# The opening of a decoder layer on one core: c as eight rows, broadcast through PE into PSUM, and a pinned order of sums, copies and splits

## The chip, the cores and the metric

The kernel runs on one core of a Trainium2 chip. The metric is device time in microseconds (us), the median of several runs. Five engines with queues of their own work side by side: PE (matrix products; its weight loads are listed apart as PEld), DVE (vector work), ACT (activations and copies), POOL, and SP, which only issues DMA transfers here. Matrix products are written into PSUM, which is divided into banks of 128 partitions by 512 float32 values. Everything else lives in SBUF.

## The reference, cut to what matters

One decoder layer over 512 tokens of width 1024. A conditioning vector c of 1024 values is multiplied by a large matrix, and the result shifts and scales the tokens. The shifted and scaled tokens u are then multiplied by one wide projection:

```python
mod = c @ w_ada + b_ada
sh1, sc1, gt1, sh2, sc2, gt2 = split(mod, 6)
u = x * (1.0 + sc1) + sh1
proj = u @ w_in          # q, k, v of two attention branches, forget logits, branch gates
...                      # two attentions, output projection, LayerNorm, gated MLP, LayerNorm
```

Only the first two parts of mod (sh1 and sc1), u, and the first columns of proj are touched by the change. All inputs and the output are float32.

## The kernel before, in words

The 1024 channels are cut into eight tiles of 128 (KT = 8). A tile j holds channels in the partitions and the 512 tokens in the free dimension. The opening runs a loop over the tiles. For a tile it needs 128 values of sh1 and 128 of sc1, one for each partition. They are sums over 1024 products of c and a row of the transposed w_ada. So c is needed in every partition, as a tile cbc of 128 x 1024.

**Where cbc comes from.** c is loaded as one row, cbr (L101, on SP's queue). PE multiplies a column of ones with it (L194), once for each half e of 512 columns, into the banks grp[0] and grp[1]. ACT copies each bank into a half of cbc (L195). Then PE runs WARM = 10 products of a tile of zeros (L197) into grp[5], whose results nobody uses.

**The first tile, j = 0.** SP issues the halves of wa[0] (rows for sh1) and wa[1] (rows for sc1) in turn (L217), then 384 columns of w1, the projection weights (L218), the tokens xt (L219), and the other 520 columns of w1 (L220). DVE makes four sums (L201; each leaves its total through a second instruction, the read of the accumulator): for each half e, both q = 0 (sh1) and q = 1 (sc1). Then it adds 1.0 to two rows of the biases bcols (L242), and adds halves and bias into modc (L245). ACT makes uh, the float32r part of u, from xt (L271). DVE makes the full u in place in xt (L282), and then ul, what uh leaves of it. The weights are split in the same way: wh by ACT (L90, the helper hi_of) and wl by DVE (L93, the helper lo_of), for j = 0 in two pieces of 384 and 520 columns. first_pad makes the second piece, and a padded tile for the eight forget columns. For j above 0, each sum is over all 1024 columns at once (mod_col), and the tile's weights are split in one piece.

**The products.** first_mm (L305) multiplies a tile's 128 channels with the columns of w1: groups g of 128 columns, each into its bank grp[g], each as three products (wh with uh, wl with uh, wh with ul), and two for the forget columns: 23 products for a tile, all accumulated over the eight tiles. For a tile, groups 0 to 4 come first, ordered by kind of product, and then groups 5 to 7. Groups 0 to 2 need the first 384 columns of w1 alone.

**What sets the order.** Instructions of one engine run in the order in which its queue holds them. SP's queue is in the order of the code. On the others, tc.issue_after(ins) puts what is traced within it behind ins on ins's engine, without a wait of its own on another engine. paced(a, b) makes a wait until b is done. Waits for data, for buffers that come free, and for a bank that another engine is using are set by the framework.

Of the kernel before, what the change touches and what calls it, by code (L numbers as in the profile page):

```python
# [8 lines left out]
F32 = mybir.dt.float32  # L9
F32R = mybir.dt.float32r  # L10
BF16 = mybir.dt.bfloat16
AF = mybir.ActivationFunctionType
ALU = mybir.AluOpType
# [3 lines left out]
P = 128  # L17
T = 512
D = 1024
KT = D // P  # L20
# [9 lines left out]
W1C = 904  # L30
# [12 lines left out]
GS = 7  # L43
SS = 10
GTILES = (3, 5, 7, 8, 12, 16, 20, 24)
WARM = 10
CUT = 5
FILL = (15, 18, 18), (11, 11, 11)


@with_exitstack
def layer_kernel(ctx: ExitStack, tc: tile.TileContext, out, xT, x, cT, crow, wa0, wa1, bcol, bgt, w1, wct, wv, bf,
                 wp, wo, lncol, lnrow, wup, cwb, wdp):
    nc = tc.nc
    ctx.enter_context(tc.manual_schedule(engines={nc.sync.engine}))
    V, S, G, PE = nc.vector, nc.scalar, nc.gpsimd, nc.tensor
# [11 lines left out]
    early = st0.enter_context(tc.tile_pool(name="early", bufs=1))  # L68
# [20 lines left out]
    def hi_of(o, i, scale=1.0):  # L89
        S.activation(o, i, AF.Copy, scale=scale)  # L90
# [6 lines left out]
        return pre.tile(shape, dt, name=s, tag=s)  # L97

    cbc = preset([P, D], F32, "cbc")
    cbr = early.tile([1, D], F32, name="cbr", tag="cbr")  # L100
    nc.sync.dma_start(cbr, crow)  # L101
    cTs = const([P, KT], F32, "cTs")
    bcols = const([P, 4, KT], F32, "bcols")
    bcd = S.dma_start(bcols, bcol)
# [3 lines left out]
    ident = const([P, P], F32, "ident")  # L108
# [80 lines left out]

    fpad = early.tile([P, KT, P], F32R, name="fpad", tag="fpad")  # L190
    G.memset(fl(fpad), 0.0)
    for e in range(2):
        c = slice(e * 512, (e + 1) * 512)
        PE.matmul(grp[e], ones[0:1, :], cbr[:, c], start=True, stop=True)  # L194
        S.activation(cbc[:, c], grp[e], AF.Copy)  # L195
    for n in range(WARM):
        PE.matmul(grp[5], warm[:, 0:P], warm, start=True, stop=True)  # L197

    def mod_sum(w, col, wt, c, e):
        o = modr[:, w, col, e : e + 1]  # L200
        state["read"] = V.scalar_tensor_tensor(wt[:, c], wt[:, c], 1.0, cbc[:, c], ALU.mult, ALU.mult, accum_out=o)  # L201
        return state["read"]

    def mod_col(w, col, wt):
# [4 lines left out]
    def first_load(j):  # L209
        wa = [early.tile([P, D], F32, name=nm("wa"), tag="wa", bufs=5) for _ in range(2)]  # L210
        r = stg.tile([P, 1024], F32, name=nm("raw"), tag="raw", bufs=LOADS)
        xt = z(F32, "xt")
        if j == 0:
            for e in range(2):
                c = slice(e * 512, (e + 1) * 512)
                for q in range(2):
                    nc.sync.dma_start(wa[q][:, c], wa0[j, q][:, c])  # L217
            nc.sync.dma_start(r[:, 0:384], w1[j][:, 0:384])  # L218
            nc.sync.dma_start(xt, xT[j * P : (j + 1) * P, :])  # L219
            nc.sync.dma_start(r[:, 384:W1C], w1[j][:, 384:W1C])  # L220
        else:
            nc.sync.dma_start(wa[0], wa0[j, 0])
            if j == 1:
                nc.sync.dma_start(wa[1], wa0[j, 1])
            nc.sync.dma_start(r[:, 0:W1C], w1[j])
            if j > 1:
                nc.sync.dma_start(wa[1], wa0[j, 1])
            nc.sync.dma_start(xt, xT[j * P : (j + 1) * P, :])
            if j == 6:
                nc.sync.dma_start(cTs, cT)  # L230
                nc.sync.dma_start(bfs, bf)
        pend[j] = [wa, xt, r]

    def first_acc(j):
        wa = pend[j][0]
        if j == 0:
            for e in range(2):
                for q in range(2):
                    s = mod_sum(q, j, wa[q], slice(e * 512, (e + 1) * 512), e)
            with tc.issue_after(s.ins):  # L240
                for q in (1, 3):
                    V.tensor_scalar_add(bcols[:, q, :], bcols[:, q, :], 1.0)  # L242
            for q in range(2):
                raw = modr[:, q, j, :]
                state["modc"] = V.scalar_tensor_tensor(modc[:, q, j : j + 1], raw[:, 0:1], raw[:, 1:2], bcols[:, q, j : j + 1], ALU.add, ALU.add)  # L245
        else:
            mod_col(0, j, wa[0])
            state["modc"] = mod_col(1, j, wa[1])

    def first_split(j):  # L250
        r = pend[j][2]
        h = stg.tile([P, 1024], F32R, name=nm("wh"), tag="wh", bufs=WBUFS)
        l = stg.tile([P, 1024], F32R, name=nm("wl"), tag="wl", bufs=WBUFS)
        hi_of(h[:, 0:W1C if j else 384], r[:, 0:W1C if j else 384])
        pend[j][2:] = [h, l, r]

    def first_pad(j):
# [9 lines left out]
    def first_mod(j):  # L267
        wa, xt = pend[j][0:2]
        sh, sc = modc[:, 0, j : j + 1], modc[:, 1, j : j + 1]
        a, b = z(F32R, "uh"), z(F32R, "ul")  # L270
        u = state["u"] = S.activation(a, xt, AF.Identity, bias=sh, scale=sc)  # L271
        if j:
            h, l, r = pend[j][2:]
            with tc.issue_after(state["modc"].ins):
                state["after"] = lo_of(l[:, 0:W1C], r[:, 0:W1C], h[:, 0:W1C])
            with tc.issue_after(u.ins):
                u = state["u"] = S.activation(xt, xt, AF.Identity, bias=sh, scale=sc)
            with tc.issue_after(state["after"].ins):
                state["after"] = lo_of(b, xt, a)
        else:  # L280
            h, l, r = pend[j][2:]
            ts = V.tensor_scalar(xt, xt, sc, sh, ALU.mult, ALU.add)  # L282
            with tc.issue_after(ts.ins):
                ts = lo_of(l[:, 0:384], r[:, 0:384], h[:, 0:384])
            with tc.issue_after(ts.ins):
                state["after"] = lo_of(b, xt, a)
        with tc.issue_after(u.ins), tc.issue_after(state["after"].ins):
            first_pad(j)
        uh.append(a)
        ul.append(b)  # L290
# [1003 lines left out]
def _pack(inputs):  # L1294
    import numpy as np

    a = {k: np.ascontiguousarray(v) for k, v in inputs.items()}
    c = np.ascontiguousarray
    w_in, w_ada = a["w_in"], a["w_ada"]
    wk = w_ada.reshape(KT, P, 6, D)  # L1300
    r = {}
    r["xT"] = c(a["x"][0].T)
    r["x"] = a["x"][0]
    r["cT"] = c(a["c"][0].reshape(KT, P).T)
    r["crow"] = a["c"]
    wt = c(w_ada.T).reshape(6, KT, P, D)
    r["wa0"] = c(wt[0:2].transpose(1, 0, 2, 3))
    kf = wk[:, :, [2, 5]].reshape(4, 2, P, 2, 2, 512).transpose(3, 4, 0, 2, 1, 5).reshape(2, 8, P, D)
    r["wa1"] = c(np.concatenate([kf[0], wt[3], wt[4], kf[1]], axis=0))
    bm = a["b_ada"].reshape(6, KT, P)  # L1310
    r["bcol"] = c(bm[[0, 1, 3, 4]].transpose(2, 0, 1))
    r["bgt"] = c(a["b_ada"].reshape(6, D)[[2, 5]])
    def col(kind, n):
        if kind in ("sb", "fox"):
            return (4104 if kind == "sb" else 3080) + n * P
        br, p = PAIRS[n]
        return 1544 * br + 512 * "qkv".index(kind) + p * P

    first = [w_in[:, s : s + P] for s in [col("q", 0), col("k", 0)] + [col("sb", j) for j in range(NG)]]
    cols = np.concatenate(first + [w_in[:, 1536:1544]], axis=1)  # L1320
    r["w1"] = c(cols.reshape(KT, P, W1C))
    wv = np.stack([w_in[:, 1024:1536], w_in[:, 2568:3080]])
    r["wv"] = c(wv.reshape(2, 4, 2, P, 512).transpose(0, 1, 3, 2, 4).reshape(2, 4, P, D))
    starts = [col(*t) for t in TILES]
    r["wct"] = c(np.stack([w_in[:, s : s + P].reshape(KT, P, P).transpose(1, 0, 2).reshape(P, D) for s in starts]))
    r["bf"] = c(a["b_forget"].reshape(NH, 1))
    wpj = np.stack([a["w_fox_proj"], a["w_sb_proj"]]).reshape(2, 4, P, 4, 2, P)
    r["wp"] = c(wpj.transpose(0, 3, 2, 4, 1, 5).reshape(2, 4, P, D))
    r["wo"] = c(a["w_o"].reshape(KT, P, D))
    r["lncol"] = c(np.stack([a["ln1_g"].reshape(KT, P), a["ln1_b"].reshape(KT, P)]).transpose(2, 0, 1))  # L1330
    r["lnrow"] = c(np.stack([a["ln1_g"], a["ln1_b"], a["ln2_g"], a["ln2_b"]]))
    wu = a["w_up"].reshape(KT, P, 2, FT, P)
    r["wup"] = c(wu.transpose(3, 2, 1, 0, 4).reshape(2 * FT, P, D))
    cwb = np.concatenate([a["conv_w"], a["conv_b"][None]], axis=0).reshape(4, 2, FT, P)
    r["cwb"] = c(cwb.transpose(3, 2, 1, 0).reshape(P, 2 * FT, 4))
    wd = a["w_down"].reshape(FP, 2, P, 2, 512)
    b11, b12, b21, b22 = [wd[:, m, :, n] for m in range(2) for n in range(2)]
    r["wdp"] = c(np.concatenate([b11, b12, b22, b21], axis=2))
    return r


_NAMES = ["xT", "x", "cT", "crow", "wa0", "wa1", "bcol", "bgt", "w1", "wct", "wv", "bf", "wp", "wo", "lncol", "lnrow",
          "wup", "cwb", "wdp"]


# [17 lines left out]
```

## Time and profile before

| What | us |
|---|---|
| Median of three runs | 742.30 |
| The three runs | 742.14, 742.30, 743.58 |
| The profiled execution, as timed | 743.61 |
| Its span, from first to last instruction | 741.8 |

Busy shares of the span: PE 98%, DVE 82%, ACT 53%, POOL 11%. A row of the profile names the engine, the line of the kernel, the operation, what it writes and reads (out<-in), the shape and the count. In a timeline the first two columns are the start and the duration in us, and the brackets at the end hold the idle time ahead of the row and who ended it. Rows that follow each other on one engine and line are merged, with their count behind an x. The end of a matmul is modelled, and includes the time until its result is out, so rows of PE overlap.

### The profile page before, as it was taken

Reading aid. Unit: us, or ns where it says so; the run is one execution under the profiler, and the core shown is the slowest. Engines: PE = TensorE matmul, PEld = TensorE weight load, DVE = VectorE, ACT = ScalarE, POOL = GpSimd, SP = SyncE. Lnnn points to the kernel's source line nnn. Section 1 sums busy time; section 2 is a strip of 40 time slices with the busy share of each in tenths; the row PEclk is TensorE's granted clock in tenths of the full one; section 3 lists DMA queues with packets and bytes.
Section 4 is the critical chain, followed back from the end, with each engine's and each line's share of the span. In section 5 each row is a group of like instructions: output and inputs, shape, how many; then the busy total and the mean of one; then the engine's idle time right before and its main releaser. Section 6 shows DMA issues by size and latency. Waiting matters only on the chain.

```text
span 741.8 us, 9838 instructions
## 1 busy us (share of the span) xinstructions
PE 730.3 (98%) x3444; PEld 608.1 (82%) x3444; DVE 608.6 (82%) x1050; ACT 390.5 (53%) x683; POOL 83.1 (11%) x134
## 2 busy tenths in 40 slices
PE   8999999999999999999999999999999999999995
PEld 5888888888888888888889888888888888888885
DVE  6869789988889886884587899988887797679995
ACT  4567457676976664542055455444454544346550
POOL 1027123525000000000000000000001001000010
PEclk9999999999999999999999999999999999999999
DMA  9943545423413241642062788577888867656733
GB/s 326 404 179 95 190 151 189 143 86 115 171 58 114 73 154 42 218 172 86 1 239 64 223 277 253 188 230 232 251 300 221 263 201 206 213 158 226 225 87 87
DMA packets 45220, 131.95 MB, mean 178 GB/s; under 512 B 5905, under 2 KB 6417, under 8 KB 45170
## 3 DMA queue, kind: packets, MB, share of 16 engines
q1 hardware_dynamic: 38610, 113.66, 44.9%
q0 software_dynamic: 3536, 9.24, 6.6%
q10 hardware_dynamic: 3024, 8.41, 3.1%
q8 instruction: 27, 0.44, 0.2%
q14 instruction: 23, 0.19, 0.1%
HBM read 118.38 MB, written 12.85 MB: 177 GB/s over the span
## 4 chain that ended last, share of the span: by engine, by line
PE 92%; DVE 4%; ACT 2%; DMA 1%; issue 1%; DVEq 0%; ACTq 0%
PE ps L134 18%; PE ps L133 18%; PE ps L132 18%; PE ps L305 5%; PE ps L1092 5%; PE ps L1094 5%; PE ps L1093 5%; PE ps L548 3%; PE ps L530 2%; PE ps L890 2%; PE ps L889 2%; PE ps L891 2%; DVE om L509 1%; PE ps L481 1%; PE ps L482 1%
## 5 line engine op out<-in xcount | busy, mean ns | idle before, releaser
L181 ACT ACTIVATE wh<-raw 128x1024 fp32r<-128x1024 f32 (+1 forms) x105 | 109.2, 1042 | 108.8 <-PE ps L133 36.3
L93 DVE TENSOR_TENSOR wl<-raw,wh 128x1024 fp32r<-128x1024 f32 (+2 forms) x114 | 134.8, 1185 | 30.5 <-ACT wh L181 30.3
L132 PE MATMUL ps<-u2h,wh 128*128 128x512 f32 (+1 forms) x376 | 141.5, 376 | 0.0
L133 PE MATMUL ps<-u2l,wh 128*128 128x512 f32 (+1 forms) x376 | 141.2, 376 | 0.0
L134 PE MATMUL ps<-u2h,wl 128*128 128x512 f32 (+1 forms) x376 | 141.2, 376 | 0.0
L132 PEld LDWEIGHTS ps<-u2h,wh 128*128 128x128 f32 x376 | 70.8, 188 | 13.2 <-issue 0.6
L134 PEld LDWEIGHTS ps<-u2h,wl 128*128 128x128 f32 x376 | 70.8, 188 | 12.8
L133 PEld LDWEIGHTS ps<-u2l,wh 128*128 128x128 f32 x376 | 70.8, 188 | 12.7
L132 PE MATMUL ps<-uh,wh 128*128 128x512 f32 x200 | 78.9, 394 | 0.0
L133 PE MATMUL ps<-ul,wh 128*128 128x512 f32 x200 | 78.2, 391 | 0.0
L134 PE MATMUL ps<-uh,wl 128*128 128x512 f32 x200 | 78.1, 391 | 0.0
L1142 ACT ACTIVATE cv<-ps,cw 128x512 f32<-128x512 f32 x44 | 34.0, 772 | 41.0 <-PE ps L134 34.5
L1143 DVE SCALAR_TENSOR_TENSOR cv<-ps,cw,cv 128x511 f32<-128x511 f32 x44 | 32.7, 744 | 17.2 <-ACT cv L1142 17.2
L134 PEld LDWEIGHTS ps<-uh,wl 128*128 128x128 f32 x200 | 37.5, 188 | 8.5 <-DVE wl L93 0.4
L132 PEld LDWEIGHTS ps<-uh,wh 128*128 128x128 f32 x200 | 37.6, 188 | 7.4
L133 PEld LDWEIGHTS ps<-ul,wh 128*128 128x128 f32 x200 | 37.6, 188 | 7.2
L510 POOL TENSOR_TENSOR pt<-pt,om 128x127 f32<-128x127 f32 (+3 forms) x32 | 41.4, 1306 | 9.8 <-DVE om L509 9.8
L160 POOL DMA_DIRECT2D raw<-in_wdp x10 | 8.9, 890 | 248.2 <-DVE ac L577 182.2
L1144 DVE SCALAR_TENSOR_TENSOR cv<-ps,cw,cv 128x510 f32<-128x510 f32 x44 | 32.7, 743 | 0.3
L1150 ACT ACTIVATE cv<-cv 128x512 f32<-128x512 f32 x22 | 13.9, 631 | 34.5 <-DVE cv L1144 34.5
L509 DVE TENSOR_TENSOR_SCAN om<-om,dg 128x127 f32<-128x127 f32 (+3 forms) x32 | 29.4, 978 | 0.7 <-ACT om L504 0.6
L1094 PE MATMUL ps<-wh,hv 128*128 128x512 f32 x72 | 28.0, 389 | 0.0
(234 smaller groups left out, 1581.7 us busy)
## 6 DMA issues: line engine op xcount, KB each, us to landing
raw<-in_wup SPq DMA_DIRECT2D x44, 512.0 KB, 5.6
raw<-in_wa SPq DMA_DIRECT2D x32, 512.0 KB, 4.5
raw<-in_wct SPq DMA_DIRECT2D x25, 512.0 KB, 4.0
raw<-in_wdp SPq DMA_DIRECT2D x20, 512.0 KB, 5.5
wa<-in_wa SPq DMA_DIRECT2D x14, 512.0 KB, 8.2
raw<-in_wdp SPq DMA_DIRECT2D x22, 256.0 KB, 5.1
raw<-t SPq DMA_DIRECT2D x22, 256.0 KB, 3.9
raw<-in_wdp POOLq DMA_DIRECT2D x10, 512.0 KB, 7.8
```

Of the source, the lines that this page charges most:

```text
L93: state["read"] = V.tensor_tensor(o, i, fl(hi), ALU.subtract)
L132: PE.matmul(ps, wh, ah, start=first, stop=False)
L133: PE.matmul(ps, wh, al, start=False, stop=False)
L134: return PE.matmul(ps, wl, ah, start=False, stop=last)
L181: state["hi"] = S.activation(h[:, 0:cols], r[:, 0:cols], AF.Copy)
L305: PE.matmul(grp[g], w, u, start=j == 0 and n == 0, stop=j == KT - 1 and n == (1 if g == 7 else 2))
L509: V.tensor_tensor_scan(d0, d0, dg[:, 513 - (e - s) : 512][:, ::-1], 0.0, ALU.mult, ALU.max)
L510: G.tensor_tensor(pt[b][:, s : e - 1], pt[b][:, s : e - 1], om[:, s + 1 : e], ALU.mult)
L1092: PE.matmul(ps, ah, bh, start=first, stop=False, skip_group_check=onto)
L1093: PE.matmul(ps, ah, bl, start=False, stop=False, skip_group_check=onto)
L1094: return PE.matmul(ps, al, bh, start=False, stop=last, skip_group_check=onto)
L1142: S.activation(t, ps, AF.Identity, bias=cw[:, n, 3:4], scale=cw[:, n, 2:3])
```

## The change

c is loaded as a tile c8s of eight rows of 128 values (c8), on ACT's queue, ahead of bcols. PE multiplies the k-th column of the identity, repeated 128 times, with the eight rows: that is row k of c8 in every partition, 128 columns of a bank. Eight such products fill grp[0] and grp[1]. The zeros' products are now three before them, five behind them, and three that wait for the third sum of tile 0, eleven in all.

For tile 0 the sums read grp[e] instead of cbc. Their order is q = 0 for both halves, then q = 1 for both. ACT copies a bank to cbc behind the sum of q = 1 that reads the same bank. The two bias rows are added ahead of the sums. The split of the first 384 columns of w1 is put behind the second copy. DVE makes uh for tile 0, right behind modc, and ACT makes the full u in xt. SP issues wa[0] whole, wa[1] in halves, then xt, and the two pieces of w1 behind it.

```diff
-WARM = 10
+WARM = 3, 5, 3
...
-    cbr = early.tile([1, D], F32, name="cbr", tag="cbr")
-    nc.sync.dma_start(cbr, crow)
+    c8s = early.tile([KT, P], F32, name="c8s", tag="c8s")
+    S.dma_start(c8s, c8)
...
-    for e in range(2):
-        c = slice(e * 512, (e + 1) * 512)
-        PE.matmul(grp[e], ones[0:1, :], cbr[:, c], start=True, stop=True)
-        S.activation(cbc[:, c], grp[e], AF.Copy)
-    for n in range(WARM):
-        PE.matmul(grp[5], warm[:, 0:P], warm, start=True, stop=True)
-
-    def mod_sum(w, col, wt, c, e):
+    def heat(n):
+        return [PE.matmul(grp[5], warm[:, 0:P], warm, start=True, stop=True) for _ in range(n)]
+
+    heat(WARM[0])
+    for k in range(KT):
+        o = grp[k // 4][:, k % 4 * P : (k % 4 + 1) * P]
+        m = PE.matmul(o, ident[0:KT, k : k + 1].broadcast_to([KT, P]), c8s, start=True, stop=True)
+    with tc.issue_after(m.ins):
+        heat(WARM[1])
+
+    def mod_sum(w, col, wt, c, e, by=None):
         o = modr[:, w, col, e : e + 1]
-        state["read"] = V.scalar_tensor_tensor(wt[:, c], wt[:, c], 1.0, cbc[:, c], ALU.mult, ALU.mult, accum_out=o)
+        state["read"] = V.scalar_tensor_tensor(wt[:, c], wt[:, c], 1.0, cbc[:, c] if by is None else by, ALU.mult, ALU.mult, accum_out=o)
...
         if j == 0:
+            nc.sync.dma_start(wa[0], wa0[j, 0])
             for e in range(2):
                 c = slice(e * 512, (e + 1) * 512)
-                for q in range(2):
-                    nc.sync.dma_start(wa[q][:, c], wa0[j, q][:, c])
+                nc.sync.dma_start(wa[1][:, c], wa0[j, 1][:, c])
+            nc.sync.dma_start(xt, xT[j * P : (j + 1) * P, :])
             nc.sync.dma_start(r[:, 0:384], w1[j][:, 0:384])
-            nc.sync.dma_start(xt, xT[j * P : (j + 1) * P, :])
             nc.sync.dma_start(r[:, 384:W1C], w1[j][:, 384:W1C])
...
         if j == 0:
-            for e in range(2):
-                for q in range(2):
-                    s = mod_sum(q, j, wa[q], slice(e * 512, (e + 1) * 512), e)
-            with tc.issue_after(s.ins):
-                for q in (1, 3):
-                    V.tensor_scalar_add(bcols[:, q, :], bcols[:, q, :], 1.0)
+            for q in (1, 3):
+                s = V.tensor_scalar_add(bcols[:, q, :], bcols[:, q, :], 1.0)
+            for q in range(2):
+                for e in range(2):
+                    c = slice(e * 512, (e + 1) * 512)
+                    with tc.issue_after(s.ins):
+                        s = mod_sum(q, j, wa[q], c, e, grp[e])
+                    if q:
+                        h = S.activation(cbc[:, c], grp[e], AF.Copy)
+                    if q and not e:
+                        for m in heat(WARM[2]):
+                            paced(m, s)
+            state["h"] = h
...
-        hi_of(h[:, 0:W1C if j else 384], r[:, 0:W1C if j else 384])
+        if j:
+            hi_of(h[:, 0:W1C], r[:, 0:W1C])
+        else:
+            with tc.issue_after(state["h"].ins):
+                hi_of(h[:, 0:384], r[:, 0:384])
...
-        u = state["u"] = S.activation(a, xt, AF.Identity, bias=sh, scale=sc)
         if j:
+            u = S.activation(a, xt, AF.Identity, bias=sh, scale=sc)
...
         else:
-            ts = V.tensor_scalar(xt, xt, sc, sh, ALU.mult, ALU.add)
+            with tc.issue_after(state["modc"].ins):
+                ts = V.tensor_scalar(a, xt, sc, sh, ALU.mult, ALU.add)
+            u = state["u"] = S.activation(xt, xt, AF.Identity, bias=sh, scale=sc)
```

More of the change, by code (lines that the diff above doesn't have):

```diff
@@ L51, in layer_kernel @@
 @with_exitstack
-def layer_kernel(ctx: ExitStack, tc: tile.TileContext, out, xT, x, cT, crow, wa0, wa1, bcol, bgt, w1, wct, wv, bf,
+def layer_kernel(ctx: ExitStack, tc: tile.TileContext, out, xT, x, cT, c8, wa0, wa1, bcol, bgt, w1, wct, wv, bf,
                  wp, wo, lncol, lnrow, wup, cwb, wdp):
@@ L236, in first_acc @@
         if j == 0:
-            for e in range(2):
-                for q in range(2):
-                    s = mod_sum(q, j, wa[q], slice(e * 512, (e + 1) * 512), e)
-            with tc.issue_after(s.ins):
-                for q in (1, 3):
-                    V.tensor_scalar_add(bcols[:, q, :], bcols[:, q, :], 1.0)
+            for q in (1, 3):
[11 more added lines that the diff above has]
+            state["h"] = h
             for q in range(2):
                 raw = modr[:, q, j, :]
-                state["modc"] = V.scalar_tensor_tensor(modc[:, q, j : j + 1], raw[:, 0:1], raw[:, 1:2], bcols[:, q, j : j + 1], ALU.add, ALU.add)
+                with tc.issue_after(s.ins):
+                    s = state["modc"] = V.scalar_tensor_tensor(modc[:, q, j : j + 1], raw[:, 0:1], raw[:, 1:2], bcols[:, q, j : j + 1], ALU.add, ALU.add)
         else:
@@ L1304, in _pack @@
     r["cT"] = c(a["c"][0].reshape(KT, P).T)
-    r["crow"] = a["c"]
+    r["c8"] = c(a["c"][0].reshape(KT, P))
     wt = c(w_ada.T).reshape(6, KT, P, D)
@@ L1339, in _pack @@
     return r
-_NAMES = ["xT", "x", "cT", "crow", "wa0", "wa1", "bcol", "bgt", "w1", "wct", "wv", "bf", "wp", "wo", "lncol", "lnrow",
+_NAMES = ["xT", "x", "cT", "c8", "wa0", "wa1", "bcol", "bgt", "w1", "wct", "wv", "bf", "wp", "wo", "lncol", "lnrow",
           "wup", "cwb", "wdp"]
```

## The prediction

> **What bounds the kernel now.** I read the page first, for the chain that ended last, and then that chain in order of time for the first microseconds, since the change touches the opening alone.
>
> ```profile
> span 741.8 us, 9838 instructions
> ...
> PE 92%; DVE 4%; ACT 2%; DMA 1%; issue 1%; DVEq 0%; ACTq 0%
> ```
>
> ```profile
> 0.74 1.59 DMA cbr<-in_crow
> 2.33 0.14 issue
> 2.47 3.75 PE ps L194 x4
> 6.21 4.38 PE ps L197 x10
> 10.59 39.89 PE ps L305 x172
> ```
>
> The end of the kernel hangs on PE (92% of the chain), and in the opening on five links: c lands at 2.33, L194 broadcasts it (2.47 to 6.21), ten warm-up products of L197 follow, and from there L305's matmuls, 23 for each of eight tiles, run without a hole past 50. Nothing but the moment at which that stream has got through its first tile can move the end, so that moment is what I work out. Next come the timelines of PE, ACT and DVE in the opening: start, duration, line, operation.
>
> ```profile
> 6.15 4.45 PE L197 MATMUL ps<-warm 128*128 128x512 bf16 x10
> 10.03 2.42 PE L305 MATMUL ps<-uh,wh 128*128 128x512 f32 x5
> ...
> 16.40 1.30 PE L305 MATMUL ps<-uh,wh 128*128 128x512 f32 x5
> ...
> 21.61 1.29 PE L305 MATMUL ps<-uh,wh 128*128 128x512 f32 x5
> ```
>
> Tile j=0's 23 matmuls end where j=1 begins, at 16.40; a tile takes 21.61 - 16.40 = 5.21 us, 0.227 a matmul. The ten warm-ups of 4.45 us are 0.43 apart (the last row end holds 0.2 of pipeline), and the first five of L305 take 2.42 where five later take 1.30: PE runs at half pace until about 12.0, though the table by stretches grants full clock there (the last but two of its columns):
>
> ```profile
> 10.00:11.00 1.00, 1.00 (x4) 0.81 (x3) 1.00 (x3) 0.07 (x1) 0.00 (x0) 1.00 1.04 423
> ```
>
> So L305 really starts 0.40 + 9 x 0.427 behind 6.15, at 10.39 (the row of 10.03 is its first one's early record).
>
> ```profile
> 4.54 0.60 ACT L195 ACTIVATE cbc<-ps 128x512 f32<-128x512 f32 x1 [1.90 <-PE ps L194]
> 6.25 0.60 ACT L195 ACTIVATE cbc<-ps 128x512 f32<-128x512 f32 x1 [1.11 <-PE ps L194]
> 7.49 0.52 ACT L90 ACTIVATE wh<-raw 128x384 fp32r<-128x384 f32 x1 [0.64 <-DMA raw<-in_w]
> 8.63 0.81 ACT L271 ACTIVATE uh<-xt,modc 128x512 fp32r<-128x512 f32 x1 [0.62 <-DVE modc L245]
> 9.35 0.62 ACT L90 ACTIVATE wh<-raw 128x520 fp32r<-128x520 f32 x1
> ```
>
> ```profile
> 6.88 0.69 DVE L201 SCALAR_TENSOR_TENSOR wa<-wa,cbc 128x512 f32<-128x512 f32 x1 [0.39 <-ACT cbc L195]
> ...
> 7.50 0.69 DVE L201 SCALAR_TENSOR_TENSOR wa<-wa,cbc 128x512 f32<-128x512 f32 x1
> ...
> 8.11 0.24 DVE L242 TENSOR_SCALAR bcols<-bcols 128x8 f32<-128x8 f32 x2
> 8.26 0.34 DVE L245 SCALAR_TENSOR_TENSOR modc<-modr,bcols 128x1 f32<-128x1 f32 x2
> 9.48 0.55 DVE L282 TENSOR_SCALAR xt<-xt,modc 128x512 f32<-128x512 f32 x1 [0.88 <-ACT uh L271]
> 9.94 0.55 DVE L93 TENSOR_TENSOR wl<-raw,wh 128x384 fp32r<-128x384 f32 x1
> 10.41 0.68 DVE L93 TENSOR_TENSOR ul<-xt,uh 128x512 fp32r<-128x512 f32 x1
> 11.02 0.69 DVE L93 TENSOR_TENSOR wl<-raw,wh 128x520 fp32r<-128x520 f32 x1
> ```
>
> Beside PE there is the second path: bank 1 of the broadcast (6.21), its copy, two sums 0.62 apart, the two bias rows, modc, uh on ACT. uh is there at 8.63 + 0.81 = 9.44, so PE's queue of warm-ups, not uh, sets the start by about 0.9 us.
>
> **The change, part by part.**
>
> *Eight rows.* The same 1,024 columns of float32 go through PE, now as 16 passes of 128 columns where L194 had four of 512. Four passes end at 6.21 with a spacing of about 0.85, so 0.213 for a quarter, if a pass's weight load hides beside the pass before it. The loads of L194, and transposes later on with loads and passes of the same width:
>
> ```profile
> L194 PEld LDWEIGHTS ps<-cbr,ones x4: 283/330/332, 2.4 to 4.3; 1*128 1x128 f32 x4
> ```
>
> ```profile
> 74.09 1.25 PE L530 MATMUL ps<-ident,pt 128*128 128x128 f32 x10
> ```
>
> The ten transposes come (1.25 - 0.27) / 9 = 0.109 apart at full pace, which is 0.22 at half pace: load and pass overlap. The bounds are 0.213 a pass and, with no overlap, 0.33 + 0.21 = 0.54; 0.33 alone is the middle, if a load can't be cut by the next. I take 0.213, nearest to the only row with short float32 passes. The Trainium skill, TensorE: Matmul & The Clock Gate, section "Part 3: Packing small matmuls — row/col tiling", speaks against it: a weight load overlaps running matmuls only when its row group differs, and all eight products here use the same rows. By that rule the second bank would be ready 16 x 0.33 = 5.3 us later; the trace disagrees, with 0.109.
>
> *Start of the products.* c8 goes out on ACT's queue when c went out on SP's. Landing takes from c's 1.59 us to the 1.8 of bcols, the only small transfer of that queue:
>
> ```profile
> bcols<-in_bcol ACTq DMA_DIRECT2D x1, 16.0 KB, 1.8
> ```
>
> I take c's, as nearest in bytes: 2.33 (bcols, behind it now, is wanted at 5 and lands near 3). The three heats before it:
>
> ```profile
> 0.86 0.27 DVE L106 MEMSET warm<- 128x256 uint32 x1 [0.86 <-PEq L1351]
> ```
>
> From 1.13 three heats at 0.43 last to about 2.45, just when c8 is there; up to 0.2 lost here would still be hidden, as shown below. So bank 0 is ready at 4.51 and bank 1 at 6.21, as now.
>
> *Sums from PSUM.* The first copy of 0.60 goes from ahead of the sums. Does a sum cost more from PSUM?
>
> ```profile
> L898 DVE SCALAR_TENSOR_TENSOR xn<-xn,ps 128x512 f32<-128x512 f32 x8 | 5.5, 686 | 17.3 <-PE ps L891 17.3
> ```
>
> 686 ns with a PSUM operand against 0.69: nothing. But the new order is q=0 for both halves, then q=1. The second sum needs bank 1, so three sums stand behind 6.21 where two stood: 6.25, 6.87, 7.48 (the old fourth began at 7.50). The copy's 0.60 is given back by one more sum of 0.62: gain 0.02. Their data: wa[0] is the first 512 KB and the old sums had as many bytes by 5.8, on an SP queue that starts one issue sooner now.
>
> *Bias rows, modc, uh.* The bias rows leave the path (8.11 to 8.26, 0.15; they hide in DVE's idle stretch before the sums, and if bcols landed late they would come back). modc runs from 8.10, uh as L282's operation on DVE from about 8.35 to 8.90 instead of ACT's to 9.44: 0.5 sooner.
>
> *Copies and splits behind the sums.* Here a new wait is made. A bank read by two engines is read by one after the other:
>
> ```profile
> 51.00 1.19 ACT L90 ACTIVATE s<-ps 64x512 fp32r<-64x512 f32 x2
> ```
>
> ```profile
> 52.22 1.39 DVE L409 SCALAR_TENSOR_TENSOR s<-ps,s 64x512 fp32r<-64x512 f32 x2 [1.09 <-ACT s L90]
> ```
>
> L409's first needs only ACT's first s (51.0 to 51.6) and still begins at 52.22, after ACT's second read of that bank. So copy 0 waits for the third sum (7.56) and runs to 8.2, copy 1 for the fourth (8.17) and runs to 8.8. Queued behind them on ACT are wh's first 384 columns (0.52: 8.7 to 9.22, was 8.01), xt in place, which also waits for uh (0.81, to 9.96), and wh's other 520 columns (0.62: to 10.49, was 9.97). raw's first part now lands behind xt:
>
> ```profile
> 3.44 0.43 SPq L219 DMA_DIRECT2D xt<-in_xT  x1
> ```
>
> ```profile
> xt<-in_xT SPq DMA_DIRECT2D x1, 256.0 KB, 5.1
> ```
>
> xt is down at 8.5 with raw's first part before it, and the two change places, so raw's lands by 8.5, in time for 8.7. On DVE: wl 9.27 to 9.82, ul 10.0 to 10.7 (after xt), wl's rest to 11.3, the sums of j=1 from 11.3 instead of 11.7.
>
> *Heats.* Eight stand between the products and L305 instead of ten: L305 starts at 6.15 + 0.40 + 7 x 0.427 = 9.53. wh (9.27) and uh (8.95) are there. Its fourth product wants the other 520 columns at 9.53 + 3 x 0.427 = 10.81; they are there at 10.5, so 0.25 is the cover of all that comes before. Then wl, ul and the rest are ahead of need by 0.5 and more.
>
> *The sum.* L305 begins 0.85 sooner, but at half pace: two of its matmuls take the place of two heats, so j=0 ends two full-pace matmuls sooner, 2 x 0.227 = **0.45 us**. For j=1, uh was there at
>
> ```profile
> 14.30 0.82 ACT L271 ACTIVATE uh<-xt,modc 128x512 fp32r<-128x512 f32 x1 [0.43 <-DVE modc L207]
> ```
>
> 15.12, and PE now wants it at 15.95: no wait. Everything behind follows PE and moves with it. So this execution, 741.8 of span and 743.61 as timed, would become 741.35 and 743.16. It lies 1.3 above the median of the three runs, 742.30; from that I subtract the same 0.45: 741.9.
>
> **The rivals.**
>
> *A, the clock turns early.* PE now works from 1.2 on almost without a hole: three heats, eight products, five heats. If this brings the full pace before 9 us, L305 can begin with wh at 9.3, runs three matmuls, and then waits for the 520 columns until 10.53; j=0 ends at 10.53 + 20 x 0.227 = 15.07, 1.33 sooner: 741.0. For it: the density. Against it: the four passes of L194 plus 5.8 us of dense heats and matmuls did not bring full pace before 12.0, so products on few rows seem not to count; and in a run whose clock had turned early before too, only 0.1 to 0.4 is left (742.0). The Trainium skill, TensorE: Matmul & The Clock Gate, section "Part 1: The HAM clock gate", has a free-running window of about 3.4 us that must be busy. Estimated from that page, the turn after dense work from 6.15 falls between 9.6 and 13.0 and differs from run to run; 12.0 here agrees, and so would runs 1.4 us apart.
>
> *B, the short passes are slow (the slower side).* At 0.33 a pass, bank 1 is ready 1.9 us later, the 520 columns at 12.4, and j=1 starts at 12.4 + 20 x 0.227 = 16.94, 0.5 later: 742.8. At 0.54 it is 5.3 later, j=1 at 20.3, 3.9 later: 746.2. It decides from 0.29 a pass (bank 1 1.2 late, columns at 11.7): there j=0 ends as now. For it: load rows of 0.33 at half pace; against it: the 0.109 above.
>
> *C, nothing arrives.* ACT's longer row (copies behind sums, xt ahead of the 520 columns) eats what the missing heats give, or the moment of the clock hides it: 742.3. For it: the columns' cover is 0.3 us only, and a stall there costs its full length; against it: nothing else in the row is late.
>
> **How the numbers follow.** Forecast 0.60 (741.9), A 0.20 (741.0), B 0.10 (0.06 at 742.8, 0.04 at 746.2), C 0.10 (742.3). The range, 740.9 to 743.3, takes in A and the milder B; its upper end is the forecast with the clock turning as late as in the profiled execution or a little later (1.4 above); B's far end is left out. About 0.2% (1.5 us, 740.8 and 743.8) is what a measurement here can tell from no change. Faster by more: 0.12, from A with a lucky set of runs and a little of the forecast. Slower by more: 0.08, B's far end and late clocks. Within: 0.80.
>
> **What would show it.** Right: bank 1's products end at about 6.2; sums at 6.25, 6.87, 7.48; copies at 7.6 and 8.2; wh at 8.7; PE's first L305 spacing from about 9.5; j=1 near 15.95 if the pace still turns at 12.0. A shows as matmuls 0.227 apart from L305's first one. B shows as products ending past 7.4. The forecast is wrong if copies of a bank run beside its sums, if c8 lands past 2.6, or if raw's first part lands past 8.7.

## The result, and the profile after

| What | before | after |
|---|---|---|
| Median of 21 runs each, same chip, us | 742.14 (741.30 to 743.67) | 743.26 (742.33 to 744.34) |
| Ratio after to before | | 1.0013, 95% interval 1.0007 to 1.0018 |
| The profiled execution as timed, and its span, us | 743.61, 741.8 | 743.45, 741.7 |

The change makes the kernel slower by 1 us, within the 0.2% that I had called no change, but on the other side of it than forecast. It also lies just within the forecast's range (740.9 to 743.3), and that is luck: the range reached so far up for a clock that turns late, which is not what happened. The profiled executions don't show the loss by their length: the one of before is 1.5 us over the median of its kernel. A second one of the kernel before, e4 below, has 741.77 and a span of 740.0, and is the better measure.

First the page of after (span, and the chain of waits by engine), as for before:

```profile
span 741.7 us, 9866 instructions
...
PE 96%; ACT 1%; DVE 1%; POOL 1%; issue 0%; DVEq 0%; ACTq 0%; POOLq 0%
```

PE still carries the chain. Then the timeline of PE in the opening (start, duration, line):

```profile
1.20 1.46 PE L193 MATMUL ps<-warm 128*128 128x512 bf16 x3 [1.20 <-DVE warm L106]
2.59 3.78 PE L198 MATMUL ps<-c8s,ident 8*128 8x128 f32 x16
6.30 3.59 PE L193 MATMUL ps<-warm 128*128 128x512 bf16 x8
9.50 1.16 PE L322 MATMUL ps<-uh,wh 128*128 128x512 f32 x3
10.51 0.84 PE L322 MATMUL ps<-uh,wl 128*128 128x512 f32 x3
11.19 0.62 PE L322 MATMUL ps<-uh,wh 128*128 128x512 f32 x2
...
15.04 1.33 PE L322 MATMUL ps<-uh,wh 128*128 128x512 f32 x5
```

The sixteen short passes follow without a hole and take 3.78 us, where the four long ones took 3.75. L322, the old L305, begins at 9.50, and j=1 at 15.04 where it had been 16.40. The timelines of DVE and ACT in the same stretch:

```profile
5.68 0.24 DVE L241 TENSOR_SCALAR bcols<-bcols 128x8 f32<-128x8 f32 x2 [4.05 <-DMA bcols<-in_bcol]
5.83 0.68 DVE L204 SCALAR_TENSOR_TENSOR wa<-wa,ps 128x512 f32<-128x512 f32 x1
...
7.66 0.68 DVE L204 SCALAR_TENSOR_TENSOR wa<-wa,ps 128x512 f32<-128x512 f32 x1
...
8.26 0.35 DVE L256 SCALAR_TENSOR_TENSOR modc<-modr,bcols 128x1 f32<-128x1 f32 x2
8.65 0.55 DVE L298 TENSOR_SCALAR uh<-xt,modc 128x512 fp32r<-128x512 f32 x1
```

```profile
7.84 1.20 ACT L248 ACTIVATE cbc<-ps 128x512 f32<-128x512 f32 x2 [4.58 <-DVE wa L204]
8.94 0.52 ACT L90 ACTIVATE wh<-raw 128x384 fp32r<-128x384 f32 x1
9.35 0.80 ACT L299 ACTIVATE xt<-xt,modc 128x512 f32<-128x512 f32 x1
10.05 0.63 ACT L90 ACTIVATE wh<-raw 128x520 fp32r<-128x520 f32 x1
```

The brackets show what the forecast had missed here: DVE stands idle for 4.05 us and is let go by bcols, which lands at 5.66 and not near 3. Everything on the two engines is 0.2 to 0.3 late, and still ahead of PE. In this execution most of that is not bcols: the second sum needs bank 1, which the products leave at 6.37 (2.59 + 3.78), and it begins at 6.44. In e1, the same kernel again, the products end as early and the sum begins at 6.64, behind a bcols of 5.86.

So the opening came, and the time went elsewhere. Set the two traces side by side on PE, matmul by matmul: from 60 to 670 us after is ahead of the first trace of before by 1.3 to 2.7 us; then it loses some 2 us in one place. The waits between 650 and 680 us (who waited for whom: us in total, times, longest), after and then before:

```profile
ACT wh L181 <- DMA raw<-t: 6.4, 1, 6.4
DVE hv L93 <- ACT hv L90: 5.7, 1, 5.7
...
PE ps L1109 <- DVE cv L1161: 1.7, 1, 1.7
```

```profile
ACT wh L181 <- DMA raw<-t: 4.2, 1, 4.2
DVE hv L93 <- ACT hv L90: 3.6, 1, 3.6
```

Before has no wait of PE there. In after, ACT gets the reload of t into raw 2.2 us later, DVE follows it, and PE waits 1.7 us for DVE's cv. The chain of after in that stretch (start, duration, what) has the same steps:

```profile
667.16 1.04 ACT wh L181
668.20 0.67 ACT cv L1159
668.87 0.53 ACT wdh L90
669.40 0.73 DVE cv L1160
...
670.64 0.75 DVE cv L1161
671.39 0.14 issue
671.53 0.47 PE ps L1109
```

In before the chain through this stretch is PE alone.

### The profile page after: what moved, and what is told of

Same layout as the page of the kernel before. It is cut to its first block, busy times and chain, and to the rows that moved or that the text cites. A ratio compares the mean times of both kernels' runs of the same rounds, so it can differ in the third digit from the quotient of the medians.

```text
span 741.7 us, 9866 instructions
## 1 busy us (share of the span) xinstructions
PE 729.4 (98%) x3457; PEld 610.0 (82%) x3457; DVE 608.6 (82%) x1050; ACT 391.2 (53%) x683; POOL 82.7 (11%) x134
## 4 chain that ended last, share of the span: by engine, by line
PE 96%; ACT 1%; DVE 1%; POOL 1%; issue 0%; DVEq 0%; ACTq 0%; POOLq 0%
PE ps L133 19%; PE ps L134 19%; PE ps L132 19%; PE ps L322 5%; PE ps L1109 5%; PE ps L1111 5%; PE ps L1110 5%; PE ps L565 3%; PE ps L547 2%; PE ps L908 2%; PE ps L907 2%; PE ps L906 2%; PE ps L475 2%; PE ps L473 2%; PE ps L474 2%; PE ps L499 1%
## 5 line engine op out<-in xcount | busy, mean ns | idle before, releaser
L133 PEld LDWEIGHTS ps<-u2l,wh 128*128 128x128 f32 x376 | 70.8, 188 | 12.6
```

Of the source, the lines that this page charges most:

```text
L133: PE.matmul(ps, wh, al, start=False, stop=False)
```

## The experiments

**Is it chance, the lead, or the order?** Where the kernel does not pin the order of ACT, DVE and PE, the framework's planner chooses it. It had given these queues another order between 46 and 80 us, far behind the change, and only where the kernel has the eight products. Theory O: that order costs the time. Rival D: the reload of t lands when it lands, and takes back any lead. Rival N: chance. Four kernels: after unchanged (e1); after with c as one row, which has the new opening and the old order behind it (e2); before with the eight rows alone, which has the new order (e3); before unchanged (e4).

In e2, against after (e3 makes the same edit the other way round, in before):

```diff
-    S.dma_start(c8s, c8)
+    S.dma_start(cbr, crow)
-    for k in range(KT):
-        o = grp[k // 4][:, k % 4 * P : (k % 4 + 1) * P]
-        m = PE.matmul(o, ident[0:KT, k : k + 1].broadcast_to([KT, P]), c8s, start=True, stop=True)
+    for e in range(2):
+        m = PE.matmul(grp[e], ones[0:1, :], cbr[:, e * 512 : (e + 1) * 512], start=True, stop=True)
```

> The changed kernel once more, unaltered, for a second profile. Theory O (the planner's order of the queues between 46 and 80 us, which the eight products flipped, costs about 2 us later on): ratio to before about 1.0013, j=1 starts near 15.0, and PE's lead over before is lost late, as in the first profile (1.66 us of waiting at 670). Rival D (a late reload of t from DRAM lands when it lands, and takes back any lead): the same ratio, and the same wait near 670. Rival N (chance: the wait near 670 was one execution's): no such wait, and the ratio is still 1.0013 from somewhere else.

> The change with everything but the eight rows: c as one row on ACT's queue, L194's two products with a bank each; heats, sums from PSUM, copies, splits and SP's order as in the changed kernel. The queues from 46 us on are in the order of before. Theory O: the opening's 1.3 us arrive at the end, about 741.0, ratio 0.998. Rival D: as the changed kernel, ratio 1.001.

> The kernel before with the eight rows alone: c8 on ACT's queue, eight products into the banks, copies and sums as before. The queues from 46 us on are in the order of the changed kernel. Theory O: the opening of before and the order's cost, about 744.3, ratio 1.003. Rival D: as before or up to 0.3 us to either side, ratio 1.000.

> The kernel before once more, for a second profile. All theories: a time within 741.3 to 743.7. It shows which waits of PE behind 46 us belong to the kernel and which to one execution: theory O expects no wait of over 1 us near 670 here.

Measured: e1 743.51, ratio 1.0013 (1.0002 to 1.0023); e2 743.0, 1.001 (1.0 to 1.002); e3 747.68, 1.0065 (1.0047 to 1.0082); e4 742.23. The late wait of PE is there in e1 (1.0 us) and e3 (1.7), not in e2 and e4. e3 is behind the first trace of before by 2 us at that point, so it had no lead to give back: rival D falls. With the wait in all three traces of kernels with eight products and in none of the others, chance is unlikely too. e3's size has another cause, on ACT's queue. Its rows in the opening:

```profile
7.74 0.52 ACT L90 ACTIVATE wh<-raw 128x384 fp32r<-128x384 f32 x1 [4.47 <-DMA raw<-in_w]
8.17 1.07 ACT L197 ACTIVATE cbc<-ps 128x512 f32<-128x512 f32 x2
11.77 0.81 ACT L273 ACTIVATE uh<-xt,modc 128x512 fp32r<-128x512 f32 x1 [2.53 <-DVE modc L247]
```

The planner put the split of wh, which waits for raw, ahead of the copies of c; sums, modc and uh come after that, and the first product with the weights (L305 of before) starts at 12.63, with PE at half pace from 13.2 to 16.6. The late start is what the change's pin of the split behind the copies prevents. e2 fits neither O (741.0 expected) nor D's reason; it is taken up again below.

**Theory F.** What else do eight products bring? They are 16 passes in place of 4, and there is one warming product more: 13 matmuls, each with its weight load, 26 instructions of PE. PE's busy row on the page counts them, before and then after:

```profile
PE 730.3 (98%) x3444; PEld 608.1 (82%) x3444; DVE 608.6 (82%) x1050; ACT 390.5 (53%) x683; POOL 83.1 (11%) x134
```

```profile
PE 729.4 (98%) x3457; PEld 610.0 (82%) x3457; DVE 608.6 (82%) x1050; ACT 391.2 (53%) x683; POOL 82.7 (11%) x134
```

The trace holds a DMA queue, q8, of a kind "instruction", with 27 pieces of 16 KB, about one for 255 of PE's 6,888 records. (A second queue of that kind, q14, has nothing between 652 and 683 us in any run.) With 26 instructions more in front, each piece should come about 2.8 us earlier against the work; that is an estimate, 26 of 255 at 27.5 us a piece. In after, one comes in among the reloads. The queues and issues of after, from 658 to 660 us and from 654 to 658.5 (KB each, median us from issue to landing):

```profile
q8 instruction: 1, 0.02, 3.0%
...
raw<-t SPq DMA_DIRECT2D x6, 256.0 KB, 6.7
```

And of before, from 662 to 664 us and from 657 to 660:

```profile
q8 instruction: 1, 0.02, 3.0%
...
raw<-t SPq DMA_DIRECT2D x6, 256.0 KB, 4.5
```

Theory F: the piece that falls into the burst of reloads delays it, and that is the wait. It predicts something odd: useless instructions in front of before must make it slower, more of them must make it as fast again, and useless instructions in front of after must make it faster.

e5, against before (e6 has thirty more of them ahead of the warm-ups, and WARM = 7):

```diff
+    for _ in range(13):
+        PE.matmul(grp[5][0:16, 0:16], warm[:, 0:16], warm[:, 0:16], start=True, stop=True)
     for e in range(2):
         c = slice(e * 512, (e + 1) * 512)
-        PE.matmul(grp[e], ones[0:1, :], cbr[:, c], start=True, stop=True)
+        m = PE.matmul(grp[e], ones[0:1, :], cbr[:, c], start=True, stop=True)
...
+    with tc.issue_after(m.ins):
         for n in range(WARM):
```

e7, against after:

```diff
-    heat(WARM[0])
+    for _ in range(14):
+        PE.matmul(grp[5][0:16, 0:16], warm[:, 0:16], warm[:, 0:16], start=True, stop=True)
...
-        heat(WARM[1])
+        heat(2)
+        for _ in range(26):
+            PE.matmul(grp[5][0:16, 0:16], warm[:, 0:16], warm[:, 0:16], start=True, stop=True)
```

> The kernel before with thirteen small products (16 columns, bf16) ahead of c's broadcast on PE, where PE has nothing to do; every other queue keeps its order. They are 26 more instructions of PE, as many as the change adds. Theory F (fetch): PE's instructions come in pieces of 256 by DMA, one about every 27 us; the change moves each piece some 3 us earlier against the work, and the one at 663 us falls among the five reloads of raw from t (issued from 657 us) and delays the second of them. So here: that piece 2 to 4 us after the first reload's issue instead of 6, the second reload 5.7 to 6.7 us from issue to landing instead of 4.5, PE waiting 1 to 1.7 us near 670 us for DVE's cv, time 743.3 to 744 (ratio 1.001 to 1.002). Rival O (the order that the planner gave ACT, DVE and PE from 46 us on, which only kernels with the eight rows have): no wait near 670 us, time 742.3 (1.000).

> The same with 43 small products and three warming products fewer, 80 more instructions of PE: by theory F the piece now falls some 3 us before the first reload, clear of the burst, so the second reload takes 4.5 us again, no wait near 670 us, and the time is the kernel before's (742.3, ratio 1.000, within 0.001) or what the clock's turn makes of it, within 0.5 us. By a rival by which more instructions of PE in front cost in themselves, it is slower than the thirteen: over 1.002. Rival O: 1.000 as well.

> The kernel after with its three warming products ahead of the eight rows and three of those behind them replaced by 40 small ones: 68 more instructions of PE, the same order on every other queue. Theory F: the piece that fell at 658.7 us falls near 651, before the first reload at 654.5; the second reload takes 4.5 us instead of 6.7, no wait near 670 us, and the time is 1 to 1.7 us below the kernel after's: 741.8 to 742.4 (ratio 0.999 to 1.000). Rival O: the wait of 1 to 1.7 us near 670 us is still there, time 743.3 to 743.6 (1.0013).

Measured: e5 743.39, 1.0015 (1.0005 to 1.0025); e6 741.65, 0.9993 (0.9985 to 1.0002); e7 742.62, 1.0013 (1.0004 to 1.0021). By their medians, thirteen idle products make before as slow as the change does, and forty-three do not. e5's waits between 650 and 680 us; in before ACT's was 4.2, and PE had none:

```profile
ACT wh L181 <- DMA raw<-t: 4.9, 1, 4.9
...
PE ps L1095 <- DVE cv L1147: 0.5, 1, 0.5
```

The wait is as F says but smaller than the 1 to 1.7 us foreseen, so in this one profile it carries half of the 1.1 us. The same profile has a larger loss that F does not name, between 440 and 455 us:

```profile
PE ps L132 <- DVE cv L1147: 1.1, 2, 0.6
```

There e5 loses 1.7 us against e6, matmul by matmul, behind a load of weights (raw from in_wdp) that lands late. e12 below loses 0.9 in the same place with no piece of instructions between 424 and 454 us, so such a loss needs no piece.

In e7 the wait at 670 us is down to 0.2, as F has it, and its time is missed. PE's matmuls run at half pace at first and then turn to full pace; the turn is read from their spacing, since the column of the granted clock shows 1.00 for this stretch. With three of the full warming products replaced behind the eight rows, the turn came at 14.1 us instead of 10 to 12, so e7 lost in the opening what it won behind. The warm-ups behind the rows have to be left as they are for a fair comparison.

**After with the piece moved, and the warm-ups in front of the rows.** e2 was still unexplained: slower by 0.7 us without the late wait. Theory H: the three warming products ahead of the broadcast make PE's clock turn later. e8 takes them from e2, e9 gives them to before, and e10 puts small ones in their place in after, all else of after kept.

The edits of e8 (against e2), e9 (against before, ahead of L194; as in e5, its ten warm-ups are also pinned behind the broadcast) and e10 (against after):

```diff
-WARM = 3, 5, 3
+WARM = 0, 5, 3
```

```diff
+    for n in range(3):
+        PE.matmul(grp[5], warm[:, 0:P], warm, start=True, stop=True)
```

```diff
-    heat(WARM[0])
+    for _ in range(33):
+        PE.matmul(grp[5][0:16, 0:16], warm[:, 0:16], warm[:, 0:16], start=True, stop=True)
```

> The kernel of the second run (after, with c as one row) without its three warming products ahead of c's broadcast, so that PE starts its first work with c as in the kernel before; nothing else moves. It is to tell what its excess of 0.7 us over before is made of, since it has no wait near 670 us. Theory H (the three early products shift the moment at which PE's clock turns to a later one): the turn lies between 9 and 12 us as before, time 741.8 to 742.2 (ratio 0.999 to 1.000), the 0.4 us of the opening now being kept. Rival (the excess lies elsewhere, in the opening's new order or behind it): 742.8 to 743.2 (1.001).

> The kernel before with three warming products ahead of c's broadcast, as after has them; its ten behind it stay. Six more instructions of PE, so the piece of instructions near 663 us comes 0.7 us earlier, still 5 us behind the first reload: no wait near 670 us. Theory H: 0.7 to 1.1 us slower than before (ratio 1.001 to 1.0015), the turn of the clock on average over 11.5 us. Rival: within 0.3 us of before (1.000 to 1.0004), c's broadcast 0.2 us later.

> The kernel after with 33 small products (16 columns) in the place of the three warming products ahead of the eight rows; everything behind stays, the eight warming products too. 60 more instructions of PE: by theory F the piece of instructions that fell at 658.7 us falls some 3 us before the first reload, and there is no wait of over 0.3 us near 670 us. With theory H as well: 741.3 to 742.0 (ratio 0.9985 to 0.9995). By F without H: 742.0 to 742.5 (1.000). By neither: 743.3 (1.0013).

Measured: e8 742.83, 1.0009 (1.0 to 1.0019); e9 742.86, 1.0009 (1.0 to 1.0017); e10 741.77, 0.9996 (0.9988 to 1.0005). e10 is after with thirty more products that compute nothing, and by the ratios 1.3 us faster than after; their intervals do not touch (that of after's second measurement, e1, does). Its waits between 650 and 680 us hold no wait of PE for cv, and its reloads take 4.6 us:

```profile
ACT wh L181 <- DMA raw<-t: 4.2, 1, 4.2
...
DVE hv L93 <- ACT hv L90: 3.6, 1, 3.6
```

```profile
raw<-t SPq DMA_DIRECT2D x6, 256.0 KB, 4.6
```

e10 also has the planner's new order between 46 and 80 us, and is not slow: theory O falls. H falls with e8, which should have won about 1 us over e2 and won 0.2; that e9 loses 0.6 is then not explained by it. e10's 741.77 is 0.2 below what F alone had given and within what F and H together had: it also takes three full warming products away, and what that is worth in after itself was not measured apart.

**The opening alone, with the piece out of the way.** e11 is e2 with 36 small products in the place of the three warming ones, e12 is e6 once more.

```diff
-    heat(WARM[0])
+    for _ in range(36):
+        PE.matmul(grp[5][0:16, 0:16], warm[:, 0:16], warm[:, 0:16], start=True, stop=True)
```

> The kernel of the second run (after, with c as one row) with 36 small products in the place of the three warming products ahead: the new opening, the order that before has behind it, and by theory F the piece of instructions some 2.5 us before the first reload, clear of it in every execution. The second run was 0.7 us slower than before though its one profile showed no wait near 670 us. Theory F wide (in part of its executions the piece, 5.9 us behind the first reload in the profiled one, falls into the burst, and the same holds less often for before): 741.2 to 741.8 (ratio 0.9985 to 0.9995), spread of the times under 2 us, and 0 to 0.5 us below the forty-three products on before, which is the opening's gain. Rival (the new opening or what is behind it costs 0.7 us in itself): 742.6 to 743.2 (1.0005 to 1.001), 0.9 us or more above the forty-three products on before.

> The kernel before with 43 small products and three warming products fewer once more, for the comparison with the row above on one chip: 741.4 to 741.9 (ratio 0.999 to 1.0), spread under 2 us, by both.

Measured: e11 742.19, 0.9995 (0.9986 to 1.0003), times from 741.66 to 743.75; e12 741.75, 0.9988 (0.998 to 0.9997). e11's median is above the expected range of times, its ratio at that range's edge, and its spread just over the 2 us expected. Against e12 the new opening with one row shows no gain (0.4 us slower, within the intervals). Against e2, whose profile had shown no wait at 670 us, the small products in front are worth 1.1 us by the ratios (1.001 to 0.9995, their intervals overlapping a little).

All profiles together, with the moments read from the trace. "Piece" is the start of the piece of instructions against the issue of the second reload, "reload" that reload from issue to landing, and "rest" the time from the start of the 61st matmul of L305 (in after L322; it lies in the third tile) to the end of the last matmul, so that the opening and the clock's turn are outside it.

| run | piece, us | reload, us | PE waits near 670, us | rest, us | ratio |
|---|---|---|---|---|---|
| before | +5.7 | 4.53 | 0 | 709.0 | 1 |
| e4 before again | +6.1 | 4.53 | 0 | 708.4 | 1 |
| e2 after, one row | +5.9 | 4.68 | 0 | 708.8 | 1.001 |
| e8 e2, none in front | +5.8 | 4.67 | 0 | 709.2 | 1.0009 |
| e9 before, three in front | +6.0 | 4.64 | 0 | 708.5 | 1.0009 |
| after | +4.2 | 6.70 | 1.7 | 709.6 | 1.0013 |
| e3 before, eight rows | +3.9 | 6.40 | 1.7 | 709.4 | 1.0065 |
| e1 after again | +3.2 | 5.75 | 1.0 | 708.6 | 1.0013 |
| e5 before, thirteen | +2.7 | 5.19 | 0.5 | 709.8 | 1.0015 |
| e6 before, forty-three | -2.4 | 4.44 | 0 | 707.5 | 0.9993 |
| e12 the same again | -3.1 | 4.43 | 0 | 708.5 | 0.9988 |
| e10 after, 33 | -3.0 | 4.55 | 0 | 707.8 | 0.9996 |
| e7 after, 34 | -3.2 | 4.95 | 0.2 | 707.8 | 1.0013 |
| e11 e2, 36 | -3.3 | 4.54 | 0 | 708.0 | 0.9995 |

Against the reload, the piece of after, e1 and e5 comes 1.5 to 3.4 us earlier than that of before and e4. In the four runs whose piece falls between 2.7 and 4.2 us behind the issue, the reload lands 2.5 us after the piece's start, each time (after: 658.68 and 661.21; e5: 660.03 and 662.57). The later the piece comes in, the later the reload, until it comes after the reload has landed, and then this reload is not delayed. A delay without a piece exists too: e7's reload takes 4.95. The mean rest is 709.4 us with the piece in the burst, 708.8 behind it and 707.9 ahead of it; within a group single runs lie up to 1.2 us apart.

**What stays open.** The group with the piece behind the burst is also slower than the one with it ahead, by 0.9 us on average, and e2, e8 and e9 are 0.5 to 0.7 us slower than before without any wait at 670 us in their profile. Matmul by matmul against e6, two places show. Between 128 and 141 us the five profiles of that group lose 0.3 to 0.9 us, and of the others only e11 loses over 0.15 (0.4); in these five another piece of instructions falls there, at 133.3 to 135.1 us, and in the others the nearest one comes between 123.5 and 131.8. At 98 us before, e2 and e8 lose 0.6 to 0.9 us, where PE waits for vv. That a piece is the cause in either place is not shown.

## Why the forecast was wrong

- **The products' pace: right.** 0.213 a pass from the second on, and no loss by 128-column loads. Rival B and the rule of the Trainium skill, TensorE: Matmul & The Clock Gate, section "Part 3: Packing small matmuls — row/col tiling", that stood with it, do not hold for these passes.
- **c8's landing: near, with more spread than forecast.** Its products begin at 2.59 behind the last warm-up in after. Where they wait for c8 itself they begin at 2.26 (e7), 2.69 (e3) and 2.84 (e10). A landing at 2.33 would have let them begin at 2.47, as c did in before; in e10 c8 is then past the 2.6 that was to show the forecast wrong.
- **Bias rows: wrong.** They were to hide in DVE's idle time, with bcols landing near 3. bcols landed at 5.66 (5.86 in e1), and the fourth sum began at 7.66 where 7.48 was forecast, in after mostly because the products began 0.12 later. The forecast's other steps follow: the copies at 7.84 instead of 7.56, wh at 8.94 instead of 8.7, the 520 columns done at 10.68 instead of 10.49. The cover of 0.3 us was not put to the test: the planner moved the products that want these columns behind three others (uh with wl), to 11.19, and there was 0.5 to spare.
- **Sums from PSUM, copies behind sums: right.** A sum every 0.61 us, and a copy not before the sum that reads its bank.
- **L305's start: right but for the later products.** The row says 9.50, but it holds an early record, as that of before did: the last warm-up begins at 9.26, and 0.43 behind it is 9.69, against 9.53 forecast. The clock's turn was to vary, as it did.
- **The gain of 0.45 us: right for the execution it was read from, not for the median one.** The table below has the clock's turn T, the moment from which the matmuls come at full pace, and the start of the 61st matmul. (e3, whose PE stood idle from 10 to 12.6, and e7 are left out.)

| opening | T, us: 61st matmul, us |
|---|---|
| before, ten warm-ups behind | 8.90: 23.56 (e4); 10.79: 24.63 (e5); 11.28: 24.45 (e9); 12.06: 24.79 |
| before, shorter warm-ups | 9.93: 23.57 (e6); 11.15: 24.10 (e12) |
| after and its variants | 9.83: 23.47 (e11); 10.05: 23.47; 10.67: 23.87 (e8); 11.52: 24.22 (e2); 11.92: 24.41 (e1); 12.26: 24.77 (e10) |

A clock that turns 1 us later costs about 0.5. At one T the new opening is 0.2 to 0.7 us ahead of ten warm-ups, around what was worked out. But against e12 and e6, whose warm-ups merely last 0.4 us less, it is ahead by 0.1 or less: what gained was the two warm-ups taken away, as the prediction's own sum has it ("two of its matmuls take the place of two heats"), not the rows, sums and copies around it. And in e4, which lies nearer to the median, the clock had turned at 8.90 and the last warm-ups had run at full pace: there 0.1 is left. I subtracted the 0.45 of a late execution from the median of all.
- **"Everything behind follows PE and moves with it": wrong, and this is the step that failed.** It took the work behind the opening for rigid. The change adds 26 instructions to PE's stream, which I had counted as time on PE and as nothing else; they move every later piece of instructions, and one of them lands in a burst of reloads that PE hangs on. Against e4, matmul by matmul, after is 1.0 us ahead from 140 to 665 us and e1 level with it. Near 670 us after loses 2.1 and e1 1.1, and both end 1.1 behind, which is what the medians differ by. In the medians e5 brings such a cost into before (1.0015) and e10 takes it out of after (0.9996); no single profile carries the whole of e5's at 670 us.
- **The rivals:** none named this. B's milder price (742.8) comes nearest, by a cause that the passes' pace excludes; C's place, ACT's longer row, cost nothing; A's early turn happened in part (T 10.05 in after), and was spent.

Of all versions only before with 43 idle products is ahead of before beyond an interval, and only in one of its two measurements (e12: 0.9988, 0.998 to 0.9997; e6: 0.9993, 0.9985 to 1.0002).

## What to carry to other kernels

An instruction has a price beside its time: it moves the moments at which the later instructions are fetched, and here a fetch in the middle of a burst of loads that an engine waits for cost up to 2.2 us of that load, hundreds of us behind the edit. When an edit's own stage comes out as forecast and the end does not, compare the two traces matmul by matmul, find the one place where the lead is lost, and test it by adding instructions that do nothing. And take a gain at the clock that the median execution has, not at that of the one that was profiled.

## What the runs showed of the hardware

- Where one piece of 16 KB of instructions fell into a burst of reloads, a reload of 256 KB took 0.7 to 2.2 us longer (5.19 to 6.70 against 4.53), and landed 2.5 us behind the piece's start, in all four cases. The piece itself took 0.94 to 0.96 us. What makes the delay longer than the piece is not shown.
- The moment at which PE's pace doubles varied between 8.90 and 12.26 us in twelve profiles with the full warm-ups or nearly so. The Trainium skill, TensorE: Matmul & The Clock Gate, section "Part 1: The HAM clock gate", gives a free-running window; the 9.6 to 13.0 that I estimated from it starts too late, by 0.7. In e7, with five full warming products behind the rows in place of eight, it was 14.1.
- Products of 16 columns came 0.025 us apart: 33 of them in a row of 0.98 us, the last one starting 0.81 behind the first.

```profile
1.19 0.98 PE L196 MATMUL ps<-warm 128*16 128x16 bf16 x33 [1.19 <-DVE warm L106]
```
